# Subtracting and summing by accumulating transfers in the MLP of a hybrid attention step

## The chip, the cores and the metric

The kernel runs on one core of one Trainium2 chip. The metric is the device time of one execution in microseconds (us). Before the change the median of three executions is 1376.64 us (1376.23 to 1377.23).

In the text the engines carry the short names of the profile: PE is TensorE (PEld its weight loads), DVE is VectorE, ACT is ScalarE, POOL is GpSimd, SP is SyncE, whose queue issues nearly all of this kernel's transfers.

## The reference

One trunk layer of a transformer is computed for two groups of 128 tokens with 2048 channels: context tokens and latent tokens. Both use the same weights, all in float32. The part that matters here is the second sub-layer, an MLP with 8192 hidden channels:

```python
def sq_relu_mlp(h, w_up, w_down):
    return jnp.square(jax.nn.relu(h @ w_up)) @ w_down

h2 = rms_norm(x, norm2_w) * (1 + sc2) + sh2
x  = x + g2 * sq_relu_mlp(h2, w_up, w_down)
```

Ahead of it stand the modulation from the conditioning vectors (`sc2`, `sh2`, `g2`), a first sub-layer with two kinds of attention, and the output projection.

## The kernel before, in words

**Steps.** The weights are streamed. Each of 456 steps loads one tile of 128 x 1024 float32 (512 KB, called `raw`) on SP's queue and multiplies with it. The list `wsteps` holds the steps in order; `run()` walks through it and emits the loads some steps ahead, then the preparation of tiles some steps ahead (`prep_to`, by `LA` or the entry of `la_at`), then the matmuls of the step, then whatever is entered in `cal` for that step (`at`). Each engine takes what is emitted for it in order and waits by semaphores.

**High and low parts.** Every float32 operand is split in two parts of the type fp32r: `hi` (tile `wH`) is a rounding copy on ACT (line 78), `lo` (tile `wL`) is the difference `raw - hi` on DVE (line 225). Each product takes three matmuls of 512 columns: hi by hi, lo by hi, hi by lo (lines 261, 262, 263). An ordinary step has 12 matmuls. A prepared tile is ready when ACT and then DVE are through with it.

**The MLP.** The hidden channels are cut into 8 pieces of two tiles of 512 (`PIECES`). For piece p + 1 `up_pair` emits 16 steps of the up projection, then `down_unit` emits 16 steps of the down projection of piece p: four units (output columns n = 0 to 3) of four steps each. So the stretch from the first down step on repeats itself every 32 steps: 16 steps down, 16 steps up. The last two pieces' down steps follow one another.

**The up pair.** Four of the eight positions of an `up_pair` (0, 2, 5 and 7, `FAST`) work with sums and differences of weight tiles, as in Strassen's scheme, in two steps x and y. `prep_x` copies the high part `XH` of the first tile; `prep_y` forms on DVE the combinations `t` (line 1008), lines 1011 to 1013, and the low parts `XL` (1015), `tL` and `uL`. `mm_x` and `mm_y` (through the helper `mm`, lines 959 to 961) multiply. The other positions are ordinary steps. At the end of the pair DVE adds up the results (tiles `up`, line 1047), ACT applies relu and square (line 1053), and after some more steps `up_T` transposes the result into the stationary tiles `aH` and `aL` of the down projection (DVE line 696). For tile 1 that transpose is emitted at the first down step.

**The sums over pieces.** Each down unit ends in two PSUM banks. For piece 0 ACT copies them to `dsum[n]`; for pieces 1 to 6 DVE adds them to `dsum[n]` (line 1086, two instructions for each unit); for piece 7 the output is formed. `gate_sum` multiplies `dsum` by the gate and adds it to the residual, three steps after the end of each unit of piece 6.

**Other work of the stretch.** DVE also computes dot products for the gate `g2` (`dots`, line 1151) at some of the steps. All 4 KB tiles come from one pool of 48 buffers (`G`), so a load waits until a buffer is free.

Of the kernel before, what the change touches and what calls it, by code (L numbers as in the profile page):

```python
# [10 lines left out]
F32 = mybir.dt.float32  # L11
# [29 lines left out]
DOT_G2 = 0, 3.2  # L41
DOT_IN = [*range(0, 10), *range(20, 30)]
PIECES = [[2 * i, 2 * i + 1] for i in range(8)]
PLACES = {4: (0, 2, 5, 7), 5: (0, 2, 4, 6, 7), 6: (0, 1, 3, 5, 6, 7), 7: (0, 1, 2, 3, 5, 6, 7), 8: range(8)}
FAST = {p: PLACES[n] for p, n in zip(range(1, 8), (4, 4, 4, 4, 4, 4, 4))}
NFAST, T_PAIR = 4, (10, 12)
LA_MLP, RL_MLP = 3, 3
LA_S = {5: 6, 4: 5, 3: 4, 2: 5, 1: 4}
CHUNKS = [2, 2, 2, 4, 6]
# [7 lines left out]
def tile_hybrid_step(ctx: ExitStack, tc: tile.TileContext, a):  # L57
# [133 lines left out]

    def add_step(src, mm, key, half=0):

        st = {"half": half, "mm": mm, "key": key, "i": len(wsteps)}
        wsteps.append(st)

        def load():
            st["raw"] = G("raw")
            sync.dma_start(st["raw"], src)
        load_at(st["i"] - LA, load)  # L200
# [16 lines left out]
    def prep(st):  # L217
# [8 lines left out]
        st.pop("raw")  # L226
        st["hl"] = tuple(st.pop(n).rearrange("p (k n) -> p k n", k=2) for n in ("hi", "lo"))

    prep_next = [0]

    def prep_to(end):
# [1 line left out]
            prep(wsteps[prep_next[0]])  # L233
            prep_next[0] += 1

    la_at, rl_at = {}, {}

    def run():
        loads.sort(key=lambda x: x[:2])
        for st in wsteps:  # L240
            while loads and loads[0][0] <= st["i"] + rl_at.get(st["i"], RL):
                loads.pop(0)[2]()
            for j in sorted(j for j in pre if j <= st["i"]):
                for fn in pre.pop(j):
                    fn()
            prep_to(st["i"] + la_at.get(st["i"], LA) + 1)
            st["mm"](st)
            st["hl"] = None
            st["mm"] = None
            for fn in cal.pop(st["i"], []):  # L250
                fn()
# [698 lines left out]
    def up_pair(p):  # L950
# [1 line left out]
        w, box, key = a["w_up"], {}, ("up", n0)  # L952
        fast = FAST[p]

        def mm(name, stat, hi, lo, l, finish=()):

            acc, f = box[name], name not in box["begun"]
            box["begun"].add(name)
            pe.matmul(acc, stat[0], hi, start=f, stop=False)  # L959
            pe.matmul(acc, stat[0], lo, start=False, stop=False)  # L960
            pe.matmul(acc, stat[1], hi, start=False, stop=l)  # L961

        def x(j, k, s):

# [16 lines left out]
        for pos, is_fast in enumerate(kinds):  # L981
            end = pos == 7
            if not is_fast:
                j = next(js)
                for i, (n, names) in enumerate(((n0, ("Q2", "Q4")), (n1, ("Q3", "Z")))):
                    lastz = not any(not k for k in kinds[pos + 1:])

                    def plain(st, j=j, names=names, lastz=lastz):
                        wh, wl = st["hl"]
                        for k in range(2):  # L990
                            for s in range(2):
                                mm(names[s], x(j, k, s), wh[:, k, :], wl[:, k, :], names[s] == "Z" and lastz and k == 1)
                    add_step(wsrc(w, 2 * j, 512 * n), plain, key)
                continue
            j = next(jf)
            b = {}

            def prep_x(b=b):
                b["XH"] = G("XH", F32R)
                copy(b["XH"], b["x"]["raw"])  # L1000

            def prep_y(b=b):
                X, Y = b["x"].pop("raw"), b["y"].pop("raw")
                b["YB"], b["XL"] = G("YB", F32R), G("XL", F32R)
                b["tH"], b["tL"], b["uH"], b["uL"] = (G(n, F32R) for n in ("tH", "tL", "uH", "uL"))
                t = G("t13")
                copy(b["YB"][:, 0:512], Y[:, 512:1024])
                dve.tensor_tensor(t.rearrange("p (a n) -> p a n", a=2), X.rearrange("p (a n) -> p a n", a=2),  # L1008
                                  Y[:, 0:512].unsqueeze(1).to_broadcast([P, 2, 512]), op=OP.add)
                copy(b["tH"], t)  # L1010
                dve.tensor_tensor(Y[:, 0:512], t[:, 0:512], X[:, 512:1024], op=OP.add)
                dve.tensor_tensor(b["YB"][:, 512:1024], Y[:, 512:1024], b["YB"][:, 0:512].bitcast(F32), op=OP.subtract)
                dve.tensor_tensor(Y[:, 512:1024], Y[:, 0:512], Y[:, 512:1024], op=OP.add)  # L1013
                copy(b["uH"], Y)
                dve.tensor_tensor(b["XL"], X, b["XH"].bitcast(F32), op=OP.subtract)
                dve.tensor_tensor(b["tL"], t, b["tH"].bitcast(F32), op=OP.subtract)
                dve.tensor_tensor(b["uL"], Y, b["uH"].bitcast(F32), op=OP.subtract)

            def mm_x(st, b=b, j=j, pos=pos, end=end):
                if pos == 0:  # L1020
                    open_banks()
                mm("Q1", x(j, 0, 0), b["XH"][:, 0:512], b["XL"][:, 0:512], end)
                if not end:
                    mm("Q3", sc(j, 3), b["XH"][:, 512:1024], b["XL"][:, 512:1024], False)

            def mm_y(st, b=b, j=j, pos=pos, end=end):
                u0, u1 = (G(f"up{n}").rearrange("p (s n) -> p s n", s=2) for n in (n0, n1)) if end else (None, None)
                if end:
                    copy(u0[:, 0, :], box["Q1"])
                lo, hi = slice(0, 512), slice(512, 1024)  # L1030
                todo = [("Q6", sc(j, 1), b["uH"][:, lo], b["uL"][:, lo]), ("Q2", x(j, 1, 0), b["YB"][:, lo], b["YB"][:, hi]),
                        ("Q7", sc(j, 2), b["tH"][:, hi], b["tL"][:, hi]), ("Q4", x(j, 1, 1), b["uH"][:, hi], b["uL"][:, hi]),
                        ("Q5", sc(j, 0), b["tH"][:, lo], b["tL"][:, lo])]
                if end:
                    todo.append(("Q3", sc(j, 3), b["XH"][:, hi], b["XL"][:, hi]))
                else:
                    todo = [todo[i] for i in ((1, 4, 3, 0, 2) if pos == 0 else (1, 4, 2, 3, 0))]
                add, sub = OP.add, OP.subtract
                post = {"Q6": [(u1[:, 0, :], u0[:, 0, :], "Q6", add)], "Q2": [(u0[:, 0, :], u0[:, 0, :], "Q2", add)],
                        "Q7": [(u1[:, 1, :], u1[:, 0, :], "Q7", add)], "Q4": [(u0[:, 1, :], u1[:, 1, :], "Q4", add)],  # L1040
                        "Q5": [(u1[:, 0, :], "Q5", u1[:, 0, :], sub), (u1[:, 1, :], "Q5", u1[:, 1, :], sub)]
                        + ([(u1[:, 1, :], u1[:, 1, :], "Z", add)] if "Z" in box else []),
                        "Q3": [(u1[:, 0, :], u1[:, 0, :], "Q3", add)]} if end else {}
                for name, stat, h, l in todo:
                    mm(name, stat, h, l, end)
                    for out, i0, i1, op in post.get(name, []):
                        dve.tensor_tensor(out, *(box[v] if isinstance(v, str) else v for v in (i0, i1)), op=op)  # L1047
                b.clear()
                if end:
                    for n, u in ((n0, u0), (n1, u1)):  # L1050
                        up_r[n] = u
                        for f in (AF.Relu, AF.Square):
                            act.activation(u.rearrange("p s n -> p (s n)"), u.rearrange("p s n -> p (s n)"), f)  # L1053
                    box.clear()

            for i, (nm, pf, mf) in enumerate((("x", prep_x, mm_x), ("y", prep_y, mm_y))):
                add_step(a["w_upF"][p - 1, j, i], mf, key)
                b[nm] = wsteps[-1]
                wsteps[-1]["prep"] = pf

    dsum = {}
    last = len(PIECES) - 1
# [12 lines left out]

    def down_unit(p, n):
        def evac(acc):
            if p == 0:
                dsum[n] = G(f"dsum{n}").rearrange("p (s n) -> p s n", s=2)
            for s in range(2):  # L1080
                if p == last:
                    out_s(acc, n, s)
                elif p == 0:
                    copy(dsum[n][:, s, :], acc[s])
                else:
                    dve.tensor_tensor(dsum[n][:, s, :], dsum[n][:, s, :], acc[s], op=OP.add)

        def stat(j):
            return lambda kk, tb: (aH[PIECES[p][j]][:, kk, tb, :], aL[PIECES[p][j]][:, kk, tb, :])
# [2 lines left out]
            return  # L1092
        unit(a["w_down"], 512 * n, [4 * j for j in PIECES[p]], stat, evac, ("down", p, n))
        if p == last - 1:
            at(end_of(("down", p, n)) + 3, lambda: gate_sum(n))

    for n in PIECES[0]:
        up_unit(n)
# [137 lines left out]
        la_at[i] = 3  # L1236
    for i in range(end_of(("up", 1)), len(wsteps)):
        la_at[i], rl_at[i] = LA_MLP, RL_MLP
        if wsteps[i]["key"][0] == "down":
            to = min([j for j in range(i, len(wsteps)) if wsteps[j]["key"][0] == "up"], default=10 ** 9) - i  # L1240
            la_at[i] = LA_S.get(to, LA_MLP)
    for i, v in LA_OUT.items():
# [89 lines left out]
```

## Time and profile before

| | before |
|---|---|
| time, median of 3 | 1376.64 us |
| profiled execution: time / span | 1376.5 / 1374.7 us |
| mean granted TensorE clock | 0.996 |
| PE busy | 1353.9 us (98%) |
| DVE busy | 1152.0 us (84%) |
| ACT busy | 682.6 us (50%) |
| POOL busy | 35.3 us (3%) |
| bytes moved by DMA | 363.42 MB, mean 264 GB/s |

The span runs from the first to the last instruction of the profiled execution; its time is 1.8 us longer. A row of groups gives line, engine, operation, output and inputs, shape, count, then busy time and the mean of one instruction in ns, then the engine's idle time before them and what ended it. In a timeline each row gives the start, the busy time, the engine, the line and the tiles; what stands in brackets is the engine's idle time before the row and what ended it. The end of a matmul is modelled, so its start is the time to read.

### The profile page before, as it was taken

The numbers are of one execution on the slowest core, as the hardware profiler recorded it, in microseconds if no ns is written. First come the engines' busy times: TensorE is split into PE (matmuls) and PEld (weight loads), VectorE is DVE, ScalarE is ACT, GpSimd is POOL, SyncE is SP. The second block draws the span as 40 slices with busy tenths as digits, with TensorE's granted clock in tenths as the row PEclk, the third lists the DMA queues.
The fourth block names the chain that finished last, engine by engine and source line by source line (L and its number), as shares of the span: only waits on it lengthen the run. The fifth ranks groups of instructions, "written<-read, shape, count | busy, mean of one in ns | idle before, by whom it ended". The sixth has DMA issues, their size and how long they took to land.

```text
span 1374.7 us, 18342 instructions
## 1 busy us (share of the span) xinstructions
PE 1353.9 (98%) x6723; PEld 1092.7 (79%) x6725; DVE 1152.0 (84%) x1499; ACT 682.6 (50%) x892; POOL 35.3 (3%) x42
## 2 busy tenths in 40 slices
PE   8999999999999999999999999999999999999998
PEld 4777787878877877888888788888878888888886
DVE  4586688978888999997869798998989999879684
ACT  4544333466546534344756565454555455555441
POOL 0000002221000000000000000000000000000000
PEclk9999999999999999999999999999999999999999
DMA  9999989856676999887466577576775776467733
GB/s 381 408 409 380 340 288 402 301 187 224 218 247 221 342 404 394 308 291 238 154 230 236 192 247 257 192 249 218 267 253 169 272 248 224 146 239 270 287 122 123
DMA packets 102986, 363.42 MB, mean 264 GB/s; under 512 B 11632, under 2 KB 12592, under 8 KB 102896
## 3 DMA queue, kind: packets, MB, share of 16 engines
q1 hardware_dynamic: 102336, 360.86, 74.1%
q8 instruction: 53, 0.87, 0.2%
q0 software_dynamic: 416, 1.31, 0.2%
q14 instruction: 37, 0.30, 0.1%
q10 hardware_dynamic: 144, 0.08, 0.0%
HBM read 356.67 MB, written 5.54 MB: 263 GB/s over the span
## 4 chain that ended last, share of the span: by engine, by line
PE 81%; DVE 9%; DMA 4%; ACT 2%; issue 2%; POOL 0%; SPq 0%; DVEq 0%; ACTq 0%; POOLq 0%
PE acc L262 14%; PE acc L263 14%; PE acc L261 14%; PE Q L960 5%; PE Q L959 5%; PE Q L961 5%; PE acc L356 4%; PE acc L357 4%; PE acc L358 4%; DVE wL L225 3%; PE ps_ada L278 3%; DMA araw<-in_w_pair 2%; DMA raw<-in_w_in 1%; PE ps_T L693 1%; DVE aT L1151 1%
## 5 line engine op out<-in xcount | busy, mean ns | idle before, releaser
L225 DVE TENSOR_TENSOR wL<-raw,wH 128x1024 fp32r<-128x1024 f32 x399 | 478.2, 1221 | 118.7 <-ACT wH L78 114.6
L78 ACT ACTIVATE wH<-raw 128x1024 fp32r<-128x1024 f32 x400 | 402.5, 1052 | 167.4 <-PE acc L262 30.3
L356 PE MATMUL acc<-wH,hH 128*128 128x512 f32 x288 | 114.6, 398 | 0.0
L357 PE MATMUL acc<-wL,hH 128*128 128x512 f32 x288 | 112.2, 390 | 0.0
L358 PE MATMUL acc<-wH,hL 128*128 128x512 f32 x288 | 112.2, 390 | 0.0
L261 PE MATMUL acc<-wH,hH 128*128 128x512 f32 x256 | 104.1, 407 | 1.9 <-ACT wH L78 1.9
L262 PE MATMUL acc<-wL,hH 128*128 128x512 f32 x256 | 101.0, 395 | 1.6 <-DVE wL L225 1.6
L263 PE MATMUL acc<-wH,hL 128*128 128x512 f32 x256 | 100.4, 392 | 0.0
L356 PEld LDWEIGHTS acc<-wH,hH 128*128 128x128 f32 x288 | 54.2, 188 | 15.5 <-issue 4.8
L78 ACT ACTIVATE tH<-t 128x1024 fp32r<-128x1024 f32 x28 | 29.8, 1063 | 72.7 <-DVE t L1008 67.5
L358 PEld LDWEIGHTS acc<-wH,hL 128*128 128x128 f32 x288 | 54.1, 188 | 11.5
L357 PEld LDWEIGHTS acc<-wL,hH 128*128 128x128 f32 x288 | 54.1, 188 | 10.6
L1151 DVE CUSTOM_DVE_ANT_0 junk<-aT,cB,cols 128x1024 bf16<-128x1024 f32 x48 | 61.7, 1285 | 0.0
L1151 DVE CUSTOM_DVE_ANT_0 aT<-aT,cB,cols 128x1024 f32<-128x1024 f32 x48 | 61.4, 1279 | 0.1
L262 PEld LDWEIGHTS acc<-wL,hH 128*128 128x128 f32 x256 | 48.5, 190 | 13.0 <-DVE wL L225 2.7
L261 PEld LDWEIGHTS acc<-wH,hH 128*128 128x128 f32 x256 | 48.5, 189 | 12.6 <-ACT wH L78 2.4
L263 PEld LDWEIGHTS acc<-wH,hL 128*128 128x128 f32 x256 | 48.5, 189 | 10.2
L278 PE MATMUL ps_ada<-araw,cpad 128*32 128x256 f32 x768 | 46.2, 382 | 2.1 <-DMA araw<-in_w_pair 1.6
L1053 ACT ACTIVATE up<-up 128x1024 f32<-128x1024 f32 x28 | 29.7, 1062 | 34.7 <-DVE up L1047 34.2
L78 ACT ACTIVATE uH<-raw 128x1024 fp32r<-128x1024 f32 x28 | 29.8, 1063 | 27.2 <-DVE raw L1013 26.3
L278 PEld LDWEIGHTS ps_ada<-araw,cpad 128*32 128x32 f32 x768 | 22.6, 109 | 23.3 <-DMA araw<-in_w_pair 5.1
L1151 DVE CUSTOM_DVE_ANT_0 aT<-aT,cB,gc_g 128x1024 f32<-128x1024 f32 x32 | 41.0, 1280 | 0.1
(597 smaller groups left out, 3183.6 us busy)
## 6 DMA issues: line engine op xcount, KB each, us to landing
raw<-in_w_in SPq DMA_DIRECT2D x136, 512.0 KB, 5.8
raw<-in_w_down SPq DMA_DIRECT2D x128, 512.0 KB, 4.4
araw<-in_w_pair SPq DMA_DIRECT2D x96, 512.0 KB, 9.0
raw<-in_w_up SPq DMA_DIRECT2D x72, 512.0 KB, 4.5
aT<-in_w_gT SPq DMA_DIRECT2D x64, 512.0 KB, 5.9
raw<-in_w_upF SPq DMA_DIRECT2D x56, 512.0 KB, 4.6
aT<-in_w_adaT SPq DMA_DIRECT2D x32, 512.0 KB, 5.4
raw<-in_w_out SPq DMA_DIRECT2D x32, 512.0 KB, 5.0
```

The source lines that it names most:

```text
L78: act.activation(out, in_, AF.Copy)
L225: dve.tensor_tensor(st["lo"], st["raw"], st["hi"].bitcast(F32), op=OP.subtract)
L261: pe.matmul(acc[tb], sh, wh[:, k, :], start=f, stop=False)
L262: pe.matmul(acc[tb], sh, wl[:, k, :], start=False, stop=False)
L263: pe.matmul(acc[tb], sl, wh[:, k, :], start=False, stop=l)
L278: pe.matmul(box["ps"][32 * k:32 * k + 32, 256 * j:256 * j + 256], cpad[:, 4 * q + k, :], raw[:, k, :], start=j == 0 and q == 0, stop=j == ...
L356: pe.matmul(acc[tb], sh, wh[:, k, :], start=kt == 0 and k == 0, stop=False)
L357: pe.matmul(acc[tb], sh, wl[:, k, :], start=False, stop=False)
L358: pe.matmul(acc[tb], sl, wh[:, k, :], start=False, stop=last and k == 1)
L959: pe.matmul(acc, stat[0], hi, start=f, stop=False)
L960: pe.matmul(acc, stat[0], lo, start=False, stop=False)
L1151: dve.tensor_tensor_reduce(out, box["raw"], cB[s, h, tag], 1.0, dst if h else baT[:, part, fb:fb + 1], OP.mult, OP.add, dst)
```

## The change

Three kinds of DVE work in the MLP are replaced by transfers on POOL's queue that add to their destination (`accum_op=OP.add`).

First, the low part of four down steps of each 32 (steps 1, 3, 5 and 7 of the 16, `LO_DMA`): `lo_dma` copies the high part on ACT, then `minus_plus` lets ACT write the negated high part into the low tile and a transfer adds the weight tile to it, read once more from DRAM. These steps are taken up two steps earlier than their neighbours (`LO_AHEAD`).

Second, the low part `XL` of each fast position of every up pair is made in the same way, out of `prep_x`. In `mm_y` the two matmuls that read `XL` move to the end of the y step, but for the last position of a pair, where they stay and the preparation of x is taken up two steps earlier instead.

Third, for output columns n = 0 and 1 (`SUM_DMA`) of pieces 1 to 6 ACT copies the two banks to a tile `part`, and a transfer adds `part` to `dsum[n]`. `gate_sum` follows five steps after the end of a unit, not three.

```diff
--- before.py
+++ after.py
@@ -41,9 +41,13 @@
 DOT_G2 = 0, 3.2
 DOT_IN = [*range(0, 10), *range(20, 30)]
 PIECES = [[2 * i, 2 * i + 1] for i in range(8)]
+LO_DMA = (1,3,5,7)
+LO_AHEAD = 2
+SUM_DMA = (0, 1)
 PLACES = {4: (0, 2, 5, 7), 5: (0, 2, 4, 6, 7), 6: (0, 1, 3, 5, 6, 7), 7: (0, 1, 2, 3, 5, 6, 7), 8: range(8)}
 FAST = {p: PLACES[n] for p, n in zip(range(1, 8), (4, 4, 4, 4, 4, 4, 4))}
-NFAST, T_PAIR = 4, (10, 12)
+NFAST = 4
+T_PAIR = 10, 12
 LA_MLP, RL_MLP = 3, 3
 LA_S = {5: 6, 4: 5, 3: 4, 2: 5, 1: 4}
 CHUNKS = [2, 2, 2, 4, 6]
@@ -191,7 +195,7 @@
 
     def add_step(src, mm, key, half=0):
 
-        st = {"half": half, "mm": mm, "key": key, "i": len(wsteps)}
+        st = {"half": half, "mm": mm, "key": key, "i": len(wsteps), "src": src}
         wsteps.append(st)
 
         def load():
@@ -226,6 +230,16 @@
         st.pop("raw")
         st["hl"] = tuple(st.pop(n).rearrange("p (k n) -> p k n", k=2) for n in ("hi", "lo"))
 
+    def minus_plus(lo, hi, src):
+
+        act.activation(lo, hi.bitcast(F32), AF.Copy, scale=-1.0)
+        pool.dma_start(lo, src.bitcast(F32R), accum_op=OP.add)
+
+    def lo_dma(st):
+        prep_hi(st)
+        st["lo"] = G("wL", F32R)
+        minus_plus(st["lo"], st["hi"], st["src"])
+
     prep_next = [0]
 
     def prep_to(end):
@@ -233,7 +247,7 @@
             prep(wsteps[prep_next[0]])
             prep_next[0] += 1
 
-    la_at, rl_at = {}, {}
+    la_at, rl_at, by_dma = {}, {}, []
 
     def run():
         loads.sort(key=lambda x: x[:2])
@@ -243,7 +257,12 @@
             for j in sorted(j for j in pre if j <= st["i"]):
                 for fn in pre.pop(j):
                     fn()
-            prep_to(st["i"] + la_at.get(st["i"], LA) + 1)
+            to = st["i"] + la_at.get(st["i"], LA) + 1
+            while by_dma and by_dma[0] < to + LO_AHEAD:
+                prep_to(by_dma[0] - LO_AHEAD)
+                st_ = wsteps[by_dma.pop(0)]
+                st_.pop("early", lambda st_=st_: lo_dma(st_))()
+            prep_to(to)
             st["mm"](st)
             st["hl"] = None
             st["mm"] = None
@@ -952,13 +971,15 @@
         w, box, key = a["w_up"], {}, ("up", n0)
         fast = FAST[p]
 
-        def mm(name, stat, hi, lo, l, finish=()):
-
-            acc, f = box[name], name not in box["begun"]
-            box["begun"].add(name)
-            pe.matmul(acc, stat[0], hi, start=f, stop=False)
-            pe.matmul(acc, stat[0], lo, start=False, stop=False)
-            pe.matmul(acc, stat[1], hi, start=False, stop=l)
+        def mm(name, stat, hi, lo, l):
+
+            todo = [(stat[0], hi), (stat[1], hi)] if lo is None else [(stat[0], lo)]
+            if hi is not None and lo is not None:
+                todo = [(stat[0], hi), (stat[0], lo), (stat[1], hi)]
+            for i, (sv, wv) in enumerate(todo):
+                f = name not in box["begun"]
+                box["begun"].add(name)
+                pe.matmul(box[name], sv, wv, start=f, stop=l and i + 1 == len(todo))
 
         def x(j, k, s):
 
@@ -996,12 +1017,13 @@
             b = {}
 
             def prep_x(b=b):
-                b["XH"] = G("XH", F32R)
+                b["XH"], b["XL"] = G("XH", F32R), G("XL", F32R)
                 copy(b["XH"], b["x"]["raw"])
+                minus_plus(b["XL"], b["XH"], b["x"]["src"])
 
             def prep_y(b=b):
                 X, Y = b["x"].pop("raw"), b["y"].pop("raw")
-                b["YB"], b["XL"] = G("YB", F32R), G("XL", F32R)
+                b["YB"] = G("YB", F32R)
                 b["tH"], b["tL"], b["uH"], b["uL"] = (G(n, F32R) for n in ("tH", "tL", "uH", "uL"))
                 t = G("t13")
                 copy(b["YB"][:, 0:512], Y[:, 512:1024])
@@ -1012,16 +1034,15 @@
                 dve.tensor_tensor(b["YB"][:, 512:1024], Y[:, 512:1024], b["YB"][:, 0:512].bitcast(F32), op=OP.subtract)
                 dve.tensor_tensor(Y[:, 512:1024], Y[:, 0:512], Y[:, 512:1024], op=OP.add)
                 copy(b["uH"], Y)
-                dve.tensor_tensor(b["XL"], X, b["XH"].bitcast(F32), op=OP.subtract)
                 dve.tensor_tensor(b["tL"], t, b["tH"].bitcast(F32), op=OP.subtract)
                 dve.tensor_tensor(b["uL"], Y, b["uH"].bitcast(F32), op=OP.subtract)
 
             def mm_x(st, b=b, j=j, pos=pos, end=end):
                 if pos == 0:
                     open_banks()
-                mm("Q1", x(j, 0, 0), b["XH"][:, 0:512], b["XL"][:, 0:512], end)
+                mm("Q1", x(j, 0, 0), b["XH"][:, 0:512], b["XL"][:, 0:512] if end else None, end)
                 if not end:
-                    mm("Q3", sc(j, 3), b["XH"][:, 512:1024], b["XL"][:, 512:1024], False)
+                    mm("Q3", sc(j, 3), b["XH"][:, 512:1024], None, False)
 
             def mm_y(st, b=b, j=j, pos=pos, end=end):
                 u0, u1 = (G(f"up{n}").rearrange("p (s n) -> p s n", s=2) for n in (n0, n1)) if end else (None, None)
@@ -1035,6 +1056,7 @@
                     todo.append(("Q3", sc(j, 3), b["XH"][:, hi], b["XL"][:, hi]))
                 else:
                     todo = [todo[i] for i in ((1, 4, 3, 0, 2) if pos == 0 else (1, 4, 2, 3, 0))]
+                    todo += [("Q1", x(j, 0, 0), None, b["XL"][:, lo]), ("Q3", sc(j, 3), None, b["XL"][:, hi])]
                 add, sub = OP.add, OP.subtract
                 post = {"Q6": [(u1[:, 0, :], u0[:, 0, :], "Q6", add)], "Q2": [(u0[:, 0, :], u0[:, 0, :], "Q2", add)],
                         "Q7": [(u1[:, 1, :], u1[:, 0, :], "Q7", add)], "Q4": [(u0[:, 1, :], u1[:, 1, :], "Q4", add)],
@@ -1057,6 +1079,8 @@
                 add_step(a["w_upF"][p - 1, j, i], mf, key)
                 b[nm] = wsteps[-1]
                 wsteps[-1]["prep"] = pf
+                if nm == "x" and end:
+                    wsteps[-1]["prep"], wsteps[-1]["early"] = lambda: None, pf
 
     dsum = {}
     last = len(PIECES) - 1
@@ -1075,15 +1099,20 @@
 
     def down_unit(p, n):
         def evac(acc):
-            if p == 0:
-                dsum[n] = G(f"dsum{n}").rearrange("p (s n) -> p s n", s=2)
+            by_pool = 0 < p < last and n in SUM_DMA
+            if p == 0 or by_pool:
+                part = G(f"dsum{n}").rearrange("p (s n) -> p s n", s=2)
             for s in range(2):
                 if p == last:
                     out_s(acc, n, s)
-                elif p == 0:
-                    copy(dsum[n][:, s, :], acc[s])
+                elif p == 0 or by_pool:
+                    copy(part[:, s, :], acc[s])
                 else:
                     dve.tensor_tensor(dsum[n][:, s, :], dsum[n][:, s, :], acc[s], op=OP.add)
+            if p == 0:
+                dsum[n] = part
+            elif by_pool:
+                pool.dma_start(dsum[n], part, accum_op=OP.add)
 
         def stat(j):
             return lambda kk, tb: (aH[PIECES[p][j]][:, kk, tb, :], aL[PIECES[p][j]][:, kk, tb, :])
@@ -1092,7 +1121,7 @@
             return
         unit(a["w_down"], 512 * n, [4 * j for j in PIECES[p]], stat, evac, ("down", p, n))
         if p == last - 1:
-            at(end_of(("down", p, n)) + 3, lambda: gate_sum(n))
+            at(end_of(("down", p, n)) + 5, lambda: gate_sum(n))
 
     for n in PIECES[0]:
         up_unit(n)
@@ -1236,7 +1265,11 @@
         la_at[i] = 3
     for i in range(end_of(("up", 1)), len(wsteps)):
         la_at[i], rl_at[i] = LA_MLP, RL_MLP
+        if "early" in wsteps[i]:
+            by_dma.append(i)
         if wsteps[i]["key"][0] == "down":
+            if (i - first_down) % 32 in LO_DMA:
+                by_dma.append(i)
             to = min([j for j in range(i, len(wsteps)) if wsteps[j]["key"][0] == "up"], default=10 ** 9) - i
             la_at[i] = LA_S.get(to, LA_MLP)
     for i, v in LA_OUT.items():
```

## The prediction

> **What bounds the kernel now.** I read the page first, for the busy shares, then the busy time of one repetition of 32 steps, then PE's own waits in the MLP, then the starts of the matmuls around these waits. The page's span and shares:
>
> ```profile
> span 1374.7 us, 18342 instructions
> PE 1353.9 (98%) x6723; PEld 1092.7 (79%) x6725; DVE 1152.0 (84%) x1499; ACT 682.6 (50%) x892; POOL 35.3 (3%) x42
> GB/s 381 408 409 380 340 288 402 301 187 224 218 247 221 342 404 394 308 291 238 154 230 236 192 247 257 192 249 218 267 253 169 272 248 224 146 239 270 287 122 123
> ```
>
> One repetition of the MLP by windows (stretch; busy time and count of PE, PEld, DVE, ACT, POOL; clock; DMA share; GB/s):
>
> ```profile
> 1020.00:1108.00 88.00, 86.84 (x389) 71.44 (x389) 81.98 (x99) 45.05 (x49) 0.00 (x0) 1.00 0.69 231
> ```
>
> PE is busy for all but about 1 us of these 88 us; DVE, at 82, is second and close. The change takes nothing from PE: it removes no matmul and adds none. So all it can win is the time in which PE waits, and PE's list of waits from 690 us to the end is short:
>
> ```profile
> PE acc L263 <- DVE a1L L696: 1.6, 1, 1.6
> PE acc L262 <- DVE wL L225: 0.8, 1, 0.8
> PE acc L261 <- DVE up L1047: 0.4, 1, 0.4
> ```
>
> All three end on DVE, and they make 2.8 us. The list is too low, because a matmul's modelled duration (0.39) is longer than the distance of two starts, so the first part of a gap is not seen as idle. The starts say more:
>
> ```profile
> 764.00 0.39 PE L262 MATMUL acc<-wL,a1H 128*128 128x512 f32 x1
> 765.96 0.50 PE L263 MATMUL acc<-wH,a1L 128*128 128x512 f32 x1 [1.57 <-DVE a1L L696]
> ...
> 940.58 0.39 PE L261 MATMUL acc<-wH,a5H 128*128 128x512 f32 x1
> 941.05 0.50 PE L262 MATMUL acc<-wL,a5H 128*128 128x512 f32 x1
> ...
> 1019.25 0.39 PE L261 MATMUL acc<-wH,a6H 128*128 128x512 f32 x1
> 1019.48 0.39 PE L262 MATMUL acc<-wL,a6H 128*128 128x512 f32 x1
> 1019.70 0.39 PE L263 MATMUL acc<-wH,a6L 128*128 128x512 f32 x1
> 1020.46 0.50 PE L261 MATMUL acc<-wH,a6H 128*128 128x512 f32 x1 [0.36 <-DVE up L1047]
> 1020.79 0.40 PE L262 MATMUL acc<-wL,a6H 128*128 128x512 f32 x1
> ...
> 1027.86 0.39 PE L263 MATMUL acc<-wH,a7L 128*128 128x512 f32 x1
> 1028.29 0.50 PE L261 MATMUL acc<-wH,a7H 128*128 128x512 f32 x1
> 1029.55 0.50 PE L262 MATMUL acc<-wL,a7H 128*128 128x512 f32 x1 [0.76 <-DVE wL L225]
> ```
>
> Undisturbed, a matmul starts 0.227 us after the last (1019.25, 1019.48, 1019.70), so an ordinary step of 12 takes 2.72 us. Everything above that is waiting: 1.73 at 764; 0.24 at 941; 0.53 at 1020; 0.20 and 1.03 at 1028 and 1029. After each gap one more matmul starts late by 0.10 (1020.46 to 1020.79). With 0.10 for each of four stalls that is 4.1 us. A few gaps of 0.1 to 0.2 that I do not show and do not count may bring it to about 5.
>
> **Where these waits come from.** The rows of DVE and ACT around the turn from the up pair to the down steps, for piece 3 (first down step at 1019.25) and, with a DVE that is on time, for piece 6:
>
> ```profile
> 1016.31 3.50 DVE L225 TENSOR_TENSOR wL<-raw,wH 128x1024 fp32r<-128x1024 f32 x3
> 1019.72 2.86 DVE L1047 TENSOR_TENSOR up<-up,Q 128x512 f32<-128x512 f32 x4
> ...
> 1022.62 2.16 ACT L1053 ACTIVATE up<-up 128x1024 f32<-128x1024 f32 x2 [6.35 <-DVE up L1047]
> ...
> 1027.19 5.79 ACT L78 ACTIVATE wH<-raw 128x1024 fp32r<-128x1024 f32 x6
> ...
> 1280.28 0.39 PE L261 MATMUL acc<-wH,a12H 128*128 128x512 f32 x1
> ...
> 1284.63 7.68 ACT L78 ACTIVATE wH<-raw 128x1024 fp32r<-128x1024 f32 x8
> ```
>
> DVE does three low parts, then gets to the sums of the up pair at 1019.72, after PE has gone on to the down steps. ACT waits 6.35 us for these sums, applies relu and square, and only at 1027.19, 7.94 us after the first down step, copies the high part of step 3, which PE wants at 8.2 us (3 x 2.72). Where DVE is on time the same point comes 4.35 us after the first down step (1280.28 to 1284.63). So a late DVE makes ACT late, and step 3 pays.
>
> **The change part by part.** The costs per instruction, from the groups of the window 757 to 1375 us:
>
> ```profile
> L225 DVE TENSOR_TENSOR wL<-raw,wH 128x1024 fp32r<-128x1024 f32 x173 | 205.0, 1220 | 27.1 <-ACT wH L78 26.2
> L1086 DVE TENSOR_TENSOR dsum<-dsum,acc 128x512 f32<-128x512 f32 x48 | 31.0, 681 | 6.6 <-PE acc L263 6.6
> L1015 DVE TENSOR_TENSOR XL<-raw,XH 128x1024 fp32r<-128x1024 f32 x24 | 29.2, 1219 | 0.0
> L78 ACT ACTIVATE wH<-raw 128x1024 fp32r<-128x1024 f32 x173 | 172.3, 1051 | 44.5 <-DVE wL L225 20.3 <-DMA raw<-in_w_down 8.7 <-PE acc L262 7.0
> L78 ACT ACTIVATE dsum<-acc 128x512 f32<-128x512 f32 x8 | 4.7, 595 | 11.7 <-PE acc L263 11.5
> ```
>
> DVE loses, in one repetition, 4 low parts of down steps and 4 `XL` at 1.22 us, and 4 sums at 0.68: 8 x 1.22 + 4 x 0.68 = 12.5 us, so 82.0 becomes 69.5 of 88. ACT gains 8 negated copies at 1.05 and 4 bank copies at 0.595: 10.8 us, so 45 becomes 56 of 88. None of this is on PE; it matters where it moves the turn.
>
> *The turn, gain.* Ahead of the sums DVE loses the low part of step 1, one of the three at 1016.31, and the `XL` before it, 2.4 us; with the lighter load before, I take the turn to fall back to the 4.35 us of piece 6. Step 3 also no longer waits for it at all: its high part, its negated copy and its transfer are now emitted at step 30 of the repetition before, ahead of relu and square. So the gaps at 941, 1020, 1028 and 1029 go: 0.24 + 0.53 + 0.20 + 1.03 + 3 x 0.10 = 2.3 us.
>
> *The first turn (764 us).* Here PE waits for `a1L`, and DVE is not late:
>
> ```profile
> 762.74 1.06 ACT L78 ACTIVATE a1H<-ps_T 128x512 fp32r<-128x512 f32 x2
> ...
> 764.01 1.28 DVE L1151 CUSTOM_DVE_ANT_0 junk<-aT,cB,cols 128x1024 bf16<-128x1024 f32 x1
> ...
> 765.22 1.28 DVE L696 TENSOR_TENSOR a1L<-ps_T,a1H 128x512 fp32r<-128x512 f32 x2
> ```
>
> ACT now does two instructions for step 5 ahead of `a1H`, in place of one for step 3: `a1H` starts 1.05 later, at 763.8, and its first half ends at 764.4. DVE no longer has step 3's low part, so the dot product moves ahead into the free time and `a1L` starts at 764.4, ends its first half at 765.1, and PE starts there and not at 765.96: about 0.75 us won, the rest of this stall stays.
>
> *ACT behind the turn, cost.* At first down step + 4.35 ACT now does the high part and the negated copy of step 5 (2.1), then the high part of step 4 (1.05), then DVE its low part (1.22): ready at 8.7, wanted at 4 x 2.72 + 0.23 = 11.1. Nothing, with 2.4 us to spare; that cover goes if the turn stays at 7.94.
>
> *The accumulating transfer, cost.* No row shows one. What shows is the landing of two stores of 256 KB on POOL's queue (line 541), and of the plain 512 KB weight loads in the MLP:
>
> ```profile
> DMA to landing us min/median/max: 2.7/3.8/4.9
> ...
> DMA to landing us min/median/max: 3.3/4.5/10.6
> ```
>
> The low bound is 3.3, a plain load at its best; the high bound 10.6, a plain load at its worst. I take the median load, 4.5, plus 0.6 for a second pass over 512 KB (524 KB at 409 GB/s, the best slice of the page, takes 1.3; the other half overlaps the first read) plus 1.3 for POOL's start and for sharing engines with the loads: 6.4 us, nearest to the median load and an estimate. Tightest is step 5: its transfer can start at 4.35 + 2.1 = 6.45 us after the first down step and is wanted at 5 x 2.72 + 0.23 = 13.83, so 7.4 us are there. Step 7 follows two copies and one more later, from 9.6 to 19.3: 9.7 us. Steps 1 and 3 and the `XL` (moved to the end of the y step) have over 10. So at 6.4 the transfer costs nothing, with 1 us to spare at step 5. [...] The plain loads here already take 4.5.
>
> *POOL and the loads.* POOL's queue is empty in this stretch (0.00 busy in the window), so nothing stands behind its waits but the next such transfer. The engines of DMA get 8 x 0.52 MB from DRAM and 1.7 x 0.52 MB from SBUF more per repetition, 58 GB/s; counted twice for the read of the destination that makes 231 + 116 = 347 GB/s, below the 409 of the page's best slice.
>
> *Sums over pieces.* ACT's copies come at the end of units 0 and 1, and `gate_sum` two steps (5.4 us) later leaves 13.6 us for the last sum: nothing on the path.
>
> The sum: 2.3 + 0.75 = 3.05 us less waiting. The profiled execution (1376.5, span 1374.7) would take 1373.4; against the median of 1376.64 that is **1373.6 us**.
>
> **The rivals.** (1) *The transfer is late: slower.* Place: step 5 of the down steps, then step 7, in the seven repetitions behind an up pair. It decides at 7.4 us from ACT's second copy to the landing. At 9 us step 5 stalls by 1.6 x 7 = 11, less 3 won: 1385. At the bound of 10.6, 3.2 x 7 + 0.9 x 7 = 29, less 3: about 1402. For it: two reads for one write, and plain loads of up to 10.6. Against it: the median of 4.5.
>
> (2) *ACT becomes the late engine: slower.* If the sums stay late and the turn stays at 7.94, step 4 is ready at 7.94 + 2.1 + 1.05 + 1.22 = 12.3, 1.2 after 11.1. In the repetitions that turn like piece 3's, five at most, that is 6 us, less the 0.75 of the first turn and 0.3 elsewhere: about 1381.6. For it: ACT waits in order for DVE's sums 6.35 us at this turn. Against it: DVE sheds 12.5 us ahead of each.
>
> (3) *Nothing is moved: same.* The stalls go back to ACT's order, not to DVE's load, and each gap is replaced by one of its size at the next step: 1375 to 1377.
>
> [...]
>
> **How the numbers follow.** A measurement of this kernel can tell about 0.2%, 2.75 us, from no change, and the forecast lies just beyond it. Forecast: 0.55, of which 0.38 beyond 2.75 us and 0.17 within it; its own range is 1371.6 (all 5 us won) to 1375. Rival 1: 0.23; rival 2: 0.12; rival 3: 0.05; rival 4: 0.05. Faster 0.38; same 0.17 + 0.05 = 0.22; slower 0.40. The range reaches from 1371.6 over the forecast, rivals 3 and 2 and the nearer half of rival 1 to 1392; beyond it lie the far half of rival 1 and half of rival 4.
>
> **What would show it.** Right: no PE gap at steps 0 to 3 of a down block, ACT's first copy behind relu and square at about 4.4 us, DVE near 70 of 88 us, accumulating transfers landing in 5 to 7.4 us. Wrong: PE waiting for a DMA at steps 5 or 7 (rival 1, 4), PE waiting for DVE `wL` at step 4 (rival 2), or landings of over 7.4 us. The prediction fails if the time leaves 1371.6 to 1392.

## The result and the profile after

The changed kernel takes 1391.24 us (median of four executions, 1390.71 to 1392.40) against 1376.43 us of the kernel before in the same comparison. The ratio is 1.0108, with a 95% interval of 1.0090 to 1.0126: 14.8 us slower. The profiled execution took 1392.4 us, its span 1390.6 us. Medians here and below leave out one execution, of the version with steps 1, 3 and 7, that took 1499.01 us at a granted clock of 0.851.

| | before | after |
|---|---|---|
| span of the profiled execution, us | 1374.7 | 1390.6 |
| PE busy, us | 1353.9 | 1359.9 |
| DVE busy, us | 1152.0 | 1079.8 |
| ACT busy, us | 682.6 | 752.8 |
| POOL busy, us | 35.3 | 94.4 |
| bytes moved, MB | 363.42 | 399.10 |

The work moved as the change says: DVE lost 72 us and ACT gained 70. One repetition, for piece 3, as a window (busy time and count of PE, PEld, DVE, ACT, POOL; clock; DMA share; GB/s), and the page's queues (packets, MB, share of the 16 engines):

```profile
1026.00:1114.00 88.00, 86.97 (x392) 71.91 (x391) 69.71 (x85) 55.42 (x61) 8.63 (x10) 1.00 0.94 296
```

```profile
q1 hardware_dynamic: 102336, 360.86, 71.0%
q0 software_dynamic: 10208, 36.97, 14.1%
```

DVE stands at 69.7 of 88 us and ACT at 55.4, as worked out. The share of the DMA engines went from 0.69 to 0.94 for 231 and 296 GB/s. The queue of the accumulating transfers takes 14.1% for 36.97 MB where the plain loads take 71.0% for 360.86 MB: 0.38 against 0.20 per cent for each MB, so a byte that is added takes about twice the engine time of a byte that is loaded. (The two queues differ too; how much of this is the adding, the version with plain loads below shows.)

What PE waits for in the MLP, from 690 us on:

```profile
PE acc L281 <- DMA wL<-in_w_down: 12.2, 6, 3.6
PE acc L280 <- ACT a1H L82: 0.5, 1, 0.5
PE acc L281 <- DVE wL L229: 0.4, 1, 0.4
PE acc L280 <- DVE up L1069: 0.3, 1, 0.3
```

The three waits for DVE of before have nearly gone, as forecast. In their place stand six waits for an accumulating transfer of a low part. Five are at down step 5 of a block, one at step 7. The chain for the block of piece 1, whose first down step starts at 845.40: ACT's rows, POOL's issue, PE's starts.

```profile
848.26 2.15 ACT L1075 ACTIVATE up<-up 128x1024 f32<-128x1024 f32 x2 [0.36 <-DVE up L1069]
850.32 1.04 ACT L82 ACTIVATE wH<-raw 128x1024 fp32r<-128x1024 f32 x1
851.40 1.06 ACT L235 ACTIVATE wL<-wH 128x1024 fp32r<-128x1024 f32 x1
...
852.75 0.87 POOL L236 DMA_DIRECT2D wL<-in_w_down  x1 [11.32 <-DMA raw<-in_w_down]
...
858.77 0.39 PE L282 MATMUL acc<-wH,a2L 128*128 128x512 f32 x1
859.00 0.39 PE L280 MATMUL acc<-wH,a2H 128*128 128x512 f32 x1
861.24 0.50 PE L281 MATMUL acc<-wL,a2H 128*128 128x512 f32 x1 [1.85 <-DMA wL<-in_w_down]
```

The turn (relu and square done, ACT's next copy starts) is at 850.32, 4.92 after the first down step; the negated copy ends at 852.46; POOL issues 0.29 us later; PE gets the low part at 861.24. That is 8.8 us from ACT's copy to its use, where the prediction had 7.4 and estimated 6.4. The issues by queue, with the median us from issue to landing:

```profile
XL<-in_w_upF POOLq DMA_DIRECT2D x28, 512.0 KB, 7.9
wL<-in_w_down POOLq DMA_DIRECT2D x28, 512.0 KB, 8.7
dsum<-dsum POOLq DMA_DIRECT2D x12, 512.0 KB, 10.0
```

After this stall PE does not return to its pace. The same stretch by windows of 1 us, the clock being the third column from the end:

```profile
861.00:862.00 1.00, 0.76 (x3) 0.66 (x4) 1.00 (x3) 0.00 (x0) 0.00 (x0) 0.89 1.05 262
862.00:863.00 1.00, 1.00 (x4) 0.81 (x3) 1.00 (x2) 0.00 (x0) 0.00 (x0) 0.50 1.06 242
863.00:864.00 1.00, 1.00 (x4) 0.71 (x4) 1.00 (x3) 0.00 (x0) 0.00 (x0) 0.50 1.00 262
864.00:865.00 1.00, 1.00 (x4) 0.81 (x3) 0.68 (x1) 0.00 (x0) 0.00 (x0) 0.50 1.05 279
865.00:866.00 1.00, 1.00 (x6) 0.80 (x5) 0.00 (x0) 0.00 (x0) 0.00 (x0) 0.90 1.11 279
```

The granted clock is 0.50 for over 3 us: two matmuls fewer start in each, 0.42 us apart (861.83 to 862.25) in place of 0.227. Three of the six stalls (pieces 1, 2 and 5) are followed by such a stretch. Counted from the starts of the matmuls, the six stalls make 13.2 us and their first matmuls after 0.6; the stretches at half the clock cost 5.2; the first turn and small gaps 2.1. Of before's 4.9 us of waits nothing else is left, so the balance is 13.8 + 5.2 + 2.1 - 4.9 = 16.2, beside the 15.9 by which the spans differ.

### The profile page after: what moved, and what is told of

Its sections match the earlier page's. It is cut to its first block, busy times and chain, and to the rows that moved or that the text cites. A ratio compares the mean times of both kernels' runs of the same rounds, so it can differ in the third digit from the quotient of the medians.

```text
span 1390.6 us, 18553 instructions
## 1 busy us (share of the span) xinstructions
PE 1359.9 (98%) x6725; PEld 1095.7 (79%) x6725; DVE 1079.8 (78%) x1419; ACT 752.8 (54%) x972; POOL 94.4 (7%) x110
## 2 busy tenths in 40 slices
DMA packets 112780, 399.10 MB, mean 287 GB/s; under 512 B 12720, under 2 KB 13680, under 8 KB 112688
## 3 DMA queue, kind: packets, MB, share of 16 engines
q1 hardware_dynamic: 102336, 360.86, 71.0%
q0 software_dynamic: 10208, 36.97, 14.1%
## 4 chain that ended last, share of the span: by engine, by line
PE 66%; issue 18%; DMA 7%; DVE 5%; ACT 2%; POOL 1%; SPq 0%; POOLq 0%; DVEq 0%; ACTq 0%
PE acc L281 12%; PE acc L280 12%; PE acc L282 12%; PE Q L982 7%; PE acc L375 5%; PE acc L376 4%; PE acc L377 4%; DMA wL<-in_w_down 3%; PE ps_ada L297 3%; DVE wL L229 2%; DMA araw<-in_w_pair 2%; DMA raw<-in_w_in 1%; PE Z L982 1%; PE ps_T L712 1%; DVE aT L1180 1%
## 5 line engine op out<-in xcount | busy, mean ns | idle before, releaser
L229 DVE TENSOR_TENSOR wL<-raw,wH 128x1024 fp32r<-128x1024 f32 x371 | 445.9, 1220 | 206.2 <-ACT wH L82 201.4
L376 PEld LDWEIGHTS acc<-wL,hH 128*128 128x128 f32 x288 | 54.1, 188 | 10.6
L82 ACT ACTIVATE dsum<-acc 128x512 f32<-128x512 f32 x32 | 18.5, 594 | 57.9 <-PE acc L282 57.0
L236 POOL DMA_DIRECT2D XL<-in_w_upF x28 | 24.3, 868 | 318.1 <-ACT XL L235 277.7
L82 ACT ACTIVATE S<-ps_ada 128x512 f32<-128x512 f32 x12 | 7.2, 598 | 65.9 <-PE ps_ada L297 65.9
```

Source lines behind the costliest of these rows:

```text
L82: act.activation(out, in_, AF.Copy)
L229: dve.tensor_tensor(st["lo"], st["raw"], st["hi"].bitcast(F32), op=OP.subtract)
L376: pe.matmul(acc[tb], sh, wl[:, k, :], start=False, stop=False)
```

## The experiments

The theory (L): PE waits at step 5, and once at step 7, because the accumulating transfer takes 8 to 10 us where 7.4 are there. The rivals: the added traffic makes everything late (T), or ACT's added copies do (A).

**Transfers at steps 1 and 3 only.**

```diff
-LO_DMA = (1,3,5,7)
+LO_DMA = (1,3)
```

> Low parts by transfer at down steps 1 and 3 only; steps 5 and 7 go back to VectorE, XL and the sums stay as in the changed kernel. Theory L (the loss is PE waiting at step 5, and once at step 7, for a transfer that takes 8 to 10 us where 7.4 are there): no PE wait for wL from in_w_down, the gains of the turn stay, 1373 to 1375 us. Rival T (the loss is the added DMA traffic in general, which makes weight loads and ScalarE late): 14 of 68 transfers are gone, so about a fifth of the 15 us comes back, 1387 to 1389. Rival A (ScalarE's added copies): 14 of 56 negated copies are gone, likewise 1387 to 1389.

Measured: 1371.69 us, ratio 0.9966 (0.9953 to 0.9979), faster than before the change, and below the 1373 expected. PE's list of waits from 690 us to the end is empty. One repetition and the landings of its low parts:

```profile
1017.00:1103.00 86.00, 86.00 (x389) 71.41 (x388) 71.32 (x86) 53.00 (x59) 6.91 (x8) 1.00 0.90 291
```

```profile
wL<-in_w_down POOLq DMA_DIRECT2D x14, 512.0 KB, 8.0
```

PE is busy for all 86 us. The transfers are not faster (8.0 us), and the DMA share is still 0.90, but steps 1 and 3 are issued ahead of the turn and have the time. 54 of 68 transfers and 42 of 56 negated copies remain, so neither T nor A is the cause by itself.

**All steps taken up one step earlier.**

```diff
-LO_AHEAD = 2
+LO_AHEAD = 3
```

> Everything as in the changed kernel, but the steps with a transfer are taken up three steps early instead of two, so that step 5's copies stand ahead of relu and square on ScalarE. Theory L: step 5's transfer starts 5 us or more earlier and lands before it is wanted; PE's waits for wL go, 1372 to 1375 us. Rivals T and A: traffic and copies are the same, so 1390 to 1392.

Measured: 1396.84 us, ratio 1.0144 (1.0128 to 1.0159). A miss for the expectation, though its first half came true: no wait for a transferred low part is left. PE now waits at the first down step:

```profile
PE acc L280 <- ACT up L82: 13.1, 5, 3.4
```

```profile
845.55 1.06 ACT L82 ACTIVATE wH<-raw 128x1024 fp32r<-128x1024 f32 x1 [4.03 <-PE Q L982]
846.64 1.06 ACT L235 ACTIVATE wL<-wH 128x1024 fp32r<-128x1024 f32 x1
847.60 1.04 ACT L82 ACTIVATE wH<-raw 128x1024 fp32r<-128x1024 f32 x1
848.55 0.58 ACT L82 ACTIVATE up<-Q 128x512 f32<-128x512 f32 x1
...
849.18 0.50 PE L280 MATMUL acc<-wH,a2H 128*128 128x512 f32 x1 [2.94 <-ACT up L82]
```

Step 5's high part, taken up that early, waits 4.03 us until PE releases a tile; behind it on ACT stands the copy that empties a PSUM bank of the up pair, and PE needs that bank for the first down step. The wait was moved, not removed: ACT's rows follow one another from 845.55 to 848.55, and the wait of 4.03 us fits a pool that has no free buffer at the turn (not tested by itself).

**No sums by transfer.**

```diff
-SUM_DMA = (0, 1)
+SUM_DMA = ()
```

> The sums over pieces all go back to VectorE; low parts and XL by transfer as in the changed kernel. Theory L: step 5 still comes too late, so most of the loss stays, 1386 to 1391 us; a few us less if the first sum's transfer, issued about 12 us into the down steps, shares the engines with step 5's. Rival T: 12 of 68 transfers go, about 1388. Rival S (the sums are what holds POOL's queue and the buffers): back to 1374 to 1377.

Measured: 1392.27 us, ratio 1.0118 (1.0101 to 1.0135), just above the 1386 to 1391 expected, with PE's waits for transferred low parts at 11.5 us in 6. The sums are not the cause.

**Low parts only.** `XL` and the sums go back to DVE, with the low part of x formed in `prep_y` as before and no early preparation.

```diff
-SUM_DMA = (0, 1)
+SUM_DMA = ()
...
-                minus_plus(b["XL"], b["XH"], b["x"]["src"])
...
+                dve.tensor_tensor(b["XL"], X, b["XH"].bitcast(F32), op=OP.subtract)
...
-                if nm == "x" and end:
-                    wsteps[-1]["prep"], wsteps[-1]["early"] = lambda: None, pf
```

> Only the low parts of down steps 1, 3, 5 and 7 by transfer; XL and the sums on VectorE as before the change. Theory L: step 5 is as late as before or later, since VectorE is less relieved ahead of the turn: 1386 to 1394 us, with landings near 8 us. Rival T: 28 of 68 transfers are left, so about 6 of the 15 us, 1381 to 1383.

Measured: 1394.04 us, ratio 1.0127 (1.0106 to 1.0148), at the upper edge of what was expected; waits for low parts 13.8 us in 6, landings of 8.5 us. With 28 of 68 transfers the loss is still whole, which speaks against T.

**No low parts by transfer.**

```diff
-LO_DMA = (1,3,5,7)
+LO_DMA = ()
```

> No low parts of down steps by transfer, XL and the sums as in the changed kernel. Theory L: no PE wait for a transfer. Step 3's high part is again behind relu and square, but VectorE is relieved of XL ahead of the turn, so the turn falls back towards 4.35 us: most of the gain stays, 1372 to 1374.5 us. If the gain of the variant with steps 1 and 3 came from those two steps alone, 1375 to 1377.

Measured: 1373.33 us, ratio 0.9976 (0.9967 to 0.9986). Of PE's waits one is left, the first turn's:

```profile
PE acc L282 <- DVE a1L L715: 1.6, 1, 1.6
```

So `XL` and the sums by themselves take away the waits of the late turns, 3.4 us. Steps 1 and 3 add the 1.6 us of the first turn: on DVE the low part of step 3, and behind it a dot product, had stood ahead of `a1L`.

**Steps 1, 3 and 7.**

```diff
-LO_DMA = (1,3,5,7)
+LO_DMA = (1,3,7)
```

> Low parts by transfer at down steps 1, 3 and 7, XL and the sums as in the changed kernel; step 5 back on VectorE. Theory L: step 7 starts about 8 to 10 us into the block and is wanted at 19.3, so landings of up to 9.5 us are just in time: 1371 to 1375 us. If step 7 is late too, 1376 to 1382. Rival T: three quarters of the low-part transfers are there, about 1386 to 1389.

Measured: 1372.73 us, ratio 0.9972 (0.9961 to 0.9983). PE waits once for a transferred low part:

```profile
PE acc L281 <- DMA wL<-in_w_down: 1.1, 1, 1.1
```

Without step 5, step 7 is in time in all blocks but one. 61 of 68 transfers and 49 of 56 negated copies remain and the loss is gone, which excludes T and A: step 5 is what costs.

**Step 5 only.**

```diff
-LO_DMA = (1,3,5,7)
+LO_DMA = (5,)
```

> Low part by transfer at down step 5 only, XL and the sums as in the changed kernel. Theory L: nearly all of the loss comes from this one step of each block, so 7 transfers do what 28 did: PE waits for wL at step 5 in six or seven blocks, 1381 to 1391 us. Rival T (traffic): 21 of 68 transfers less, back by a third, about 1386, but with no wait at step 5 longer than elsewhere.

Measured: 1391.59 us, ratio 1.0107 (1.0090 to 1.0123): the time is just above the 1381 to 1391 expected, and for another reason. The four longest of PE's six kinds of wait:

```profile
PE acc L281 <- DMA wL<-in_w_down: 5.2, 2, 2.9
PE acc L281 <- DVE wL L229: 3.4, 6, 0.8
PE acc L282 <- DVE a1L L715: 1.9, 1, 1.9
PE acc L280 <- ACT wH L82: 1.7, 3, 0.8
```

Two waits for the transfer, not six, and 5.2 of 14.3 us in all. Most of the rest is ACT's order: step 5's two copies now stand ahead of step 3's high part, which is wanted at once. These earlier waits also put the use of step 5 back, in pieces 1, 2, 3 and 5 from 13.8 to 14.9 us or more after the first down step, so the transfer is in time there.

```profile
1032.05 1.04 ACT L82 ACTIVATE wH<-raw 128x1024 fp32r<-128x1024 f32 x1
1033.12 1.06 ACT L235 ACTIVATE wL<-wH 128x1024 fp32r<-128x1024 f32 x1
1034.09 2.94 ACT L82 ACTIVATE wH<-raw 128x1024 fp32r<-128x1024 f32 x3
...
1036.45 0.50 PE L281 MATMUL acc<-wL,a7H 128*128 128x512 f32 x1 [0.76 <-DVE wL L229]
```

In the changed kernel step 3 is ready early by its own transfer, so this cost does not arise there. Rival A thus has a place where it decides, but it is not this change's. This run alone does not show that step 5's transfer makes the loss; the version that leaves out step 5 only, above, does.

**Plain loads in place of accumulating ones.**

```diff
-        pool.dma_start(lo, src.bitcast(F32R), accum_op=OP.add)
+        pool.dma_start(lo, src.bitcast(F32R))
```

> The changed kernel with its 56 transfers for low parts as plain loads in place of accumulating ones: ScalarE's negated copy is written and then overwritten by the weight tile, so the low parts are left out and their places hold the whole weights. All instructions, issues and waits stay. Theory L with the second read as its cost: landings fall from 8.7 to about 6 us, step 5 is in time but for the late turns, 1372 to 1378 us. Rival P (the time goes to POOL's issue and the way through its queue, not to the adding): landings stay at 8 to 9 us and the time at 1388 to 1392.

Measured: 1376.28 us, ratio 1.0001 (0.9991 to 1.0010), in the upper half of what was expected. This version leaves out the low parts, so only its time is of use. The queue, the landings, the waits:

```profile
q0 software_dynamic: 10208, 36.97, 9.3%
...
XL<-in_w_upF POOLq DMA_DIRECT2D x28, 512.0 KB, 5.4
wL<-in_w_down POOLq DMA_DIRECT2D x28, 512.0 KB, 5.9
```

```profile
PE acc L281 <- DMA wL<-in_w_down: 1.8, 3, 1.2
```

The same issues on the same queue land after 5.9 us without the adding and after 8.7 with it. Those 2.8 us are the price of the adding at the median (0.3 of it in POOL's issue, which takes 0.54 in place of 0.87), and with them go 15.0 of the 1391.24 us (1391.24 - 1376.28). The queue's share falls from 14.1% to 9.3%, though its 12 sums still add. All of ACT's copies and all of POOL's issues are still there, so rivals A and P are excluded as the cause. Three short waits for transferred low parts are left even so, 1.8 us: in the blocks of pieces 1 and 5 the slack is not enough even for a plain copy. With waits for `a1H` (0.5) and for DVE's `wL` (0.4) they make the larger part of the 4.6 us by which the time stays above that of the version with steps 1 and 3.

**Dot products away from the turn.**

```diff
-DOT_IN = [*range(0, 10), *range(20, 30)]
+DOT_IN = [*range(10, 30)]
```

> The changed kernel with its dot products for the gate, and so their 512 KB loads, moved from steps 0 to 9 and 20 to 29 of each 32 to steps 10 to 29. Theory L with crowded transfer engines as the reason for the long landings (the share of the transfer engines reads 1.03 around step 5): with about three loads less around the turn, step 5's transfer lands in 6.5 to 7.5 us after ScalarE's copy in place of 8.3 to 9.7, and the waits for wL halve: 1378 to 1386 us. Rival I (an accumulating transfer takes its 8 to 9 us whatever runs beside it): landings and waits as in the changed kernel, 1388 to 1393 us.

Measured: 1412.17 us, ratio 1.0254 (1.0225 to 1.0284), a miss. The landing at step 5 does fall to about where the expectation said. For piece 2, whose first down step is at 938.25:

```profile
947.32 1.06 ACT L235 ACTIVATE wL<-wH 128x1024 fp32r<-128x1024 f32 x1
...
955.55 0.50 PE L281 MATMUL acc<-wL,a4H 128*128 128x512 f32 x1 [1.90 <-DMA wL<-in_w_down]
```

From the end of the negated copy to the use it takes 7.2 us. Over the seven blocks the low part of step 5 lands 6.2 to 9.1 us after the copy, median 7.1; in the changed kernel 6.6 to 9.7, median 8.7. But the copy itself ends 10.1 us after the first down step, since the turn is late with the dot products now on DVE in the up pair; the waits for low parts stay at 11.7 us and new ones for DVE and ACT come in. The shorter landing fits a transfer that depends on what runs beside it, but does not show it: the issue moved too, and over all 28 low parts the median landing is 8.6 us against 8.7. The time cannot be read from this run for one cause alone.

**More fast positions on the freed DVE.** Steps 1 and 3, and five fast positions of eight.

```diff
-LO_DMA = (1,3,5,7)
+LO_DMA = (1,3)
-... (4, 4, 4, 4, 4, 4, 4))}
+... (5, 5, 5, 5, 5, 5, 5))}
-NFAST = 4
+NFAST = 5
```

> The variant with transfers at down steps 1 and 3, XL and the sums, and in addition five fast positions of eight in each up pair instead of four, which takes 3 matmuls of 0.227 us out of each of seven pairs: 4.8 us. If VectorE and ScalarE keep up, 1366 to 1368 us; if the turn falls behind again, 1370 to 1378.

Measured: 1388.15 us, ratio 1.0088 (1.0073 to 1.0103), a miss.

```profile
PE Q L982 <- DMA XL<-in_w_upF: 9.0, 6, 2.4
```

Here the transfers for `XL` are the late ones: with a fast position beside the last one, whose x is taken up early, their transfers come close together (POOL issues two of them at 833.86 and 835.89, ahead of a wait that ends at 845.62). That this is what makes them late was not tested by itself. The best version found is the one with steps 1 and 3, 1371.69 us.

## Why the prediction was wrong

The forecast of 1373.6 us had the wrong sign. The measured time lies within the stated range of 1371.6 to 1392 only because that range reaches over the rivals, up to the nearer half of rival 1; the forecast's own range ended at 1375.

**Right: what bounds the kernel and what can be won.** PE's waits on DVE were put at 4.1 to 5 us; the version with steps 1 and 3 wins 4.7 to 5.0 (0.9966 of 1376.73) and leaves PE without a wait. The turn fell back to 4.3 to 4.9 us in five of seven blocks, DVE to 69.7 against 69.5 forecast, ACT to 55.4 against 56. The gaps at 941, 1020, 1028 and 1029 are gone, and the first turn kept about 1 us, as worked out, though half of it is now a wait for ACT's `a1H`.

**Right: the place.** Step 5 was named as the tightest, with the transfer to start 6.45 us after the first down step; in the blocks of pieces 0, 3 and 6 ACT's copy ends at 6.47. The decision point of 7.4 us held where the turn was near its forecast place: 8.8 us stalls in piece 1, and piece 4, where the low part lands 6.6 us after the copy's end, has no stall at step 5. Piece 0 has none at 9.2 us: there the transposes of tile 1 and the waits of the first turn put the use back to 15.8 us after the first down step, 0.2 after the landing.

**Wrong: the size of the transfer.** The term of the sum that failed is 6.4 us for an accumulating transfer. It measured 8.7 at the median. One part of it was mis-sized: the second pass, put at 0.6 us, half of it hidden behind the first. The other parts, 4.5 for a plain load and 1.3 for POOL's start and the sharing of the engines, which no run shows by itself, make 5.8, and the same transfers without the adding landed after 5.9. The adding itself costs 2.8, and 5.8 + 2.8 is 8.6. The 0.6 us were worked out from the best slice of the page and an assumed overlap; no row of before showed a transfer that adds. The prediction's own high bound, 10.6 us, covered it; the value taken did not. The profile before also had a slower pair of stores on POOL's queue than the one it showed, on line 559, with landings of 4.0 to 6.9 us.

Why the adding takes 2.8 us is in part open. The prediction judged the crowd by the mean of a repetition, 347 of 409 GB/s, and the engines are fuller than that around step 5:

```profile
845.00:862.00 17.00, 15.15 (x67) 12.24 (x66) 11.17 (x15) 13.97 (x15) 2.59 (x3) 0.99 1.03 328
```

But the share of the engines does not put the landings of step 5 in order. From POOL's issue to the landing, for pieces 1, 4 and 5:

```profile
852.75:861.19 8.44, 6.63 (x30) 5.16 (x28) 7.19 (x10) 7.42 (x9) 2.59 (x3) 1.00 1.02 315
1121.43:1127.72 6.29, 6.29 (x30) 5.17 (x28) 5.01 (x7) 6.26 (x8) 2.59 (x3) 1.00 0.95 277
1211.29:1219.97 8.68, 4.72 (x20) 3.26 (x18) 3.67 (x3) 5.79 (x7) 2.59 (x3) 1.00 0.79 205
```

It takes 8.4 us at a share of 1.02, 6.3 at 0.95 and 8.7 at 0.79. That a crowd makes the adding dear is not shown.

**Wrong: two things left out.** In the blocks of pieces 2 and 5 the turn was still late, 6.8 and 7.9 us after the first down step, where the sum took 4.35 for all, and step 5 stalled by 3 to 4 us there. Rival 2 had such a late turn, but charged it to step 4 only. The largest stall, in piece 5, with its first down step at 1200.99:

```profile
1204.28 2.16 ACT L1075 ACTIVATE up<-up 128x1024 f32<-128x1024 f32 x2 [4.46 <-DVE up L1069]
...
1209.94 1.06 ACT L235 ACTIVATE wL<-wH 128x1024 fp32r<-128x1024 f32 x1
...
1220.02 0.67 PE L281 MATMUL acc<-wL,a10H 128*128 128x512 f32 x1 [3.58 <-DMA wL<-in_w_down]
```

And the half clock after three of the stalls, 5.2 us, was in no rival. Rival 1 had 11 us of stalls at 9 us and 1385; with the 13.2 us that were counted and the half clock, 1385 + 2.2 + 5.2 is 1392.4, the time of the profiled execution. That they meet to the tenth is luck, since the parts are rounded. So rival 1 was the case that came, with its mechanism, its place and its point of decision, but it was held at 0.23 against 0.55.

**The other rivals.** ACT as the late engine (2) shows in the two late turns, but PE's waits for DVE's `wL` are 0.4 us in all. That nothing is moved (3) is excluded. Rival 4, that DVE's work holds up POOL's transfers, does not show: with DVE busy for 70 of 88 us each of the 28 issues of a low part takes 0.86 or 0.87 us, as in the row at 852.75.

## What to carry to other kernels

A transfer that adds to its destination is not priced by a plain one: here 512 KB landed 2.8 us later with the adding than without (8.7 against 5.9), and a byte took about twice the engine time of a plain load's (0.38 against 0.20 per cent of the engines for each MB; 0.25 on the same queue with 56 of the 68 adding transfers made plain). Where the slack is of the size of the estimate, as here with 1 us to spare beside an estimate of 6.4, the high bound is the value to plan with. Off-loading an engine by transfers paid here where the transfer could be issued well ahead (steps 1 and 3, `XL`, the sums: 1371.69 us) and turned into a loss at the one step where it could not (step 5, without which the time is 1372.73 us and with which it is 1391.24), so the tightest consumer decided and not the sum of what was taken away. To start such a step earlier was no free cure here: its first copy waited 4.03 us for a tile, the emptying of a PSUM bank stood behind it on ACT, and PE waited for ACT at the first down step instead, 13.1 us in 5 waits (1396.84 us).

## What the runs showed of the hardware

In the MLP of the changed kernel the granted clock reads 0.50 from 861.78, 953.94 and 1220.18 on, each time for 3.41 us, and 1.00 in the rest. Windows of that length around the stalls of pieces 1 and 6 (second number from the left the length, then PE's busy time):

```profile
858.37:861.78 3.41, 1.56 (x7) 1.00 (x6) 3.41 (x6) 1.84 (x2) 0.16 (x1) 1.00 1.04 306
861.78:865.19 3.41, 3.41 (x9) 2.65 (x8) 2.90 (x4) 0.00 (x0) 0.00 (x0) 0.50 1.05 261
...
1305.51:1308.92 3.41, 2.50 (x12) 1.73 (x10) 2.41 (x3) 3.03 (x4) 0.87 (x1) 1.00 1.07 276
1308.92:1312.34 3.42, 2.13 (x9) 1.79 (x10) 1.25 (x2) 0.00 (x0) 0.00 (x0) 1.00 1.04 261
1312.34:1315.75 3.41, 3.41 (x16) 2.83 (x16) 0.00 (x0) 0.00 (x0) 0.00 (x0) 1.00 1.06 276
```

The gap of 2.24 us between two starts in piece 1 (859.00 to 861.24), in which PE is idle for 1.85 us, is followed by 3.41 us at half the clock. The longer gap of 2.59 us in piece 6 (1307.62 to 1310.21), with 2.20 us idle, is not: the clock stays at 1.00. Nor is a gap of 3.30 us in the version with step 5 only (1128.43 to 1131.73, 2.92 us idle), behind which the clock reads 1.00 up to 1135. So the length of a gap alone did not decide in these runs; what did was not shown.
